# A decoder layer on one core: a fifth pair by seven products in three chunks, and VectorE's queue issued by an account of its time

## The chip, the cores and the metric

The kernel runs on one core of a Trainium2 chip. The metric is the device time of one execution in microseconds. The kernel before takes 1052.63 us (median of three runs, 1052.0 to 1052.91).

The core has five engines that run their own queues in order: TensorE (PE; PEld is its loading of weights), VectorE (DVE), ScalarE (ACT), GpSimd (POOL) and SyncE (SP). SP and POOL mostly issue DMAs here. An engine waits for another by semaphores, and an instruction that waits holds up what stands behind it in the queue of its engine.

## The reference

One decoder layer for 256 tokens of width 2048, in float32:

```python
h   = RMSNorm_pre(x)
p   = h @ W_in                          # A.q A.k A.v | c_q | c_kv | k_rope
A   = dilated sliding-window attention  # 8 heads x 128
B   = multi-head latent attention       # 8 heads
x   = x + RMSNorm_post(concat(A, B) @ W_out)
h   = RMSNorm_pre2(x)
u   = square(relu(h @ W_up))            # W_up is 2048 x 8192
x   = x + RMSNorm_post2(u @ W_down)     # W_down is 8192 x 2048
```

The change is in the up projection, `h @ W_up`.

## The kernel before

**Three products for one.** Each float32 operand is split into a high part `hi` (ScalarE rounds it, line 306 or 310) and a rest `lo` (VectorE subtracts, line 307 or 311). A product is then three matmuls, hi x hi, hi x lo and lo x hi (`three`, line 1048). Each weight tile is loaded from memory by a DMA on SP (line 188), split, and used.

**The up projection** runs over eight chunks `j` of 1024 columns of `W_up`. The 2048 rows of the sum are sixteen blocks `k` of 128 rows. A plain step `k` multiplies one block with both halves of the tokens (`b`) and both halves of the columns (`n`): 4 products, 12 matmuls. Two neighbouring blocks `2k` and `2k+1` form a pair, which is a 2 x 2 by 2 x 2 product of blocks; `seven_products` (line 1053) does it with seven block products, 21 matmuls, in place of eight, 24. For this it needs sums of the weight blocks (called `t` and `u`) and sums of the left blocks (`left_sums`, line 1023, by VectorE and ScalarE, once for the whole projection). The partial results `m` are put together once per chunk (`close`, line 1067) and added to the accumulators (line 967).

`UP_STEPS` (line 105) says what is done in each chunk: `k` is a plain step, `w` a pair whose weight sums VectorE computes on the spot (lines 359 to 364), `p` a prepared pair, whose sums DMAs have computed in memory during the earlier stages (`prepare`, line 583: two copies issued on SP, then four accumulating DMAs on POOL). The sums of a prepared pair come back through the buffer `tu` (1 MB, issued on POOL, line 433) in chunks 0 to 4 and as ordinary loads from chunk 5 on. In chunk 0 all steps are plain, in chunks 1 to 5 pairs 0 to 3 go by seven products (0 and 2 prepared), in chunks 6 and 7 pairs 0 to 2.

The gain of the second norm is multiplied into the weights where they are split (line 310 with a scale, line 311), or, for the blocks that pairs use, into the left side in `left_sums`; `SCALED` (line 110) lists those blocks.

**What sets the order.** All queues are filled in the order in which the Python program issues instructions. `Flow` (line 126) is a planner with a clock of its own: every matmul adds its cost (line 296), and chains of other work (evacuation, sums, prepares) are generators that yield a delay and go on when the clock has come to that time (`pump`). `prepare_all` starts at 50 us of this clock and issues a prepare about every 25. This clock decides only the order in the queues; on the chip each engine goes as fast as its semaphores let it.

`Weights` (line 167) issues load and split of a tile ahead of its use: `get(i)` issues everything up to tile `i + 6` (`W_AHEAD`), but no more than the 8 buffers of `hi` and `lo` allow. Functions hung on a tile (`first`) run when it is issued: the sums of a `w` pair, the loads of `ab` and `tu`. At a chunk's end `up_evac` (line 964) adds `more` to the accumulator on VectorE (967), takes the relu on ScalarE (971), transposes on TensorE (300, tile `rt`) and squares on ScalarE (989). VectorE's addition stands in its queue behind all splits that `get` has issued by then.

Of the kernel before, what the change touches and what calls it, by code (L numbers as in the profile page):

```python
# [26 lines left out]
P = 128  # L27
# [68 lines left out]
SUMS_AHEAD, LOAD_AHEAD = 2, 3  # L96
NUP = FF // CW
# [68 lines left out]

class Weights:


    def __init__(self, nc, pool, split, bufs, ahead):  # L170
        self.nc, self.pool, self.split_fn = nc, pool, split
        self.bufs, self.limit, self.ahead = bufs, bufs, ahead
        self.specs, self.tiles, self.done = [], [], []
        self.first, self.queue = {}, {}

# [46 lines left out]
    def get(self, i):  # L222
        self.emit(i + 1 + self.ahead)
        return self.tiles[i]

# [38 lines left out]
def layer(nc, tc, io):  # L264
    flow = Flow()

# [36 lines left out]
    def split(hi, lo, src, g=None):  # L303
        if g is not None:
            return split_gain(hi, lo, src, g)
        nc.scalar.activation(hi, src, AF.Copy)  # L306
        nc.vector.tensor_tensor(out=lo, in0=src, in1=hi.bitcast(F32), op=OP.subtract)  # L307

    def split_gain(hi, lo, src, g):
        nc.scalar.activation(hi, src, AF.Copy, scale=g)  # L310
        nc.vector.scalar_tensor_tensor(  # L311
# [35 lines left out]
    def seven(load, targets):  # L347
# [3 lines left out]
        st, tt, H = {}, nc.vector.tensor_tensor, 512  # L351
# [159 lines left out]
    def rstd_of(ss, n, width, name, by=None):  # L511
# [4 lines left out]
        nc.vector.tensor_scalar(t, ss, s, e, op0=OP.mult, op1=OP.add)  # L516
# [15 lines left out]
    if N_WARM:  # L532
        zero = mix.tile([P, 512], BF16, name="zero")
        nc.vector.memset(zero, 0.0)
# [28 lines left out]
    def prelude():  # L563
# [14 lines left out]
        nc.vector.reduce_sum(ss0, ss0h, axis=mybir.AxisListType.X)  # L578
# [27 lines left out]
    def tables():  # L606
# [6 lines left out]
        nc.vector.tensor_copy(pos_f, pos_i)  # L613
        ang = pa.tile([P, 2, NB, 96], F32, tag="qkT", bufs=2, name="ang")
        kk_ = pa.tile([P, 2, NB, 96], F32, tag="qkT", bufs=2, name="kk_")
        for w in range(2):
            for b in range(NB):
                nc.vector.tensor_scalar_mul(ang[:, w, b, :], freq[:, w * 96:(w + 1) * 96], pos_f[:, b:b + 1])
            nc.vector.tensor_scalar(kk_[:, w], ang[:, w], 1.0 / (2 * np.pi), 0.25 * w, op0=OP.mult, op1=OP.add)
        yield 1.0  # L620
        nc.vector.tensor_scalar(kk_, kk_, MAGIC, -MAGIC, op0=OP.add, op1=OP.add)
        for c in (C1, C2, C3):
            nc.vector.scalar_tensor_tensor(out=ang, in0=kk_, scalar=-c, in1=ang, op0=OP.mult, op1=OP.add)
        yield 1.0
        nc.vector.tensor_scalar_add(ang[:, 1], ang[:, 1], float(np.pi / 2))
        nc.vector.tensor_scalar(ang, ang, PI_LO, -PI_LO, op0=OP.min, op1=OP.max)
# [3 lines left out]
    def rope(tmp_pool, dst, src, half, nh, first, name):  # L630
# [8 lines left out]
        nc.vector.tensor_tensor(out=t1, in0=src, in1=table(1, 0, w), op=OP.mult)  # L639
        nc.vector.tensor_tensor(out=t2[:, :, :, :half], in0=src[:, :, :, half:], in1=table(0, 0, half), op=OP.mult)  # L640
        nc.vector.tensor_tensor(out=t2[:, :, :, half:], in0=src[:, :, :, :half], in1=table(0, half, w), op=OP.mult)
        nc.vector.tensor_tensor(out=dst, in0=t1, in1=t2, op=OP.add)

    def softmax_pv(wk, dl, sc, bias, scale, v, head, name):
# [4 lines left out]
        for i, (a, e, m) in enumerate(spans):  # L649
            nc.vector.tensor_tensor_reduce(  # L650
                out=s[:, a:e], in0=sc[:, a:e], in1=m, op0=OP.add, op1=OP.max, scale=1.0,
                scalar=-3e38, accum_out=st[:, i:i + 1])
        nc.vector.tensor_scalar_mul(st[:, 2:4], st[:, 0:2], -scale)
# [5 lines left out]
        nc.vector.reciprocal(st[:, 6:8], st[:, 4:6])  # L659
        for i, (a, e, m) in enumerate(spans):  # L660
            nc.vector.tensor_scalar_mul(s[:, a:e], s[:, a:e], st[:, 6 + i:7 + i])
# [13 lines left out]
    def heads_a(qkv, half, hs, after):  # L675
        while any(c in flow.chains for c in after):
            yield 0.5
        for h in hs:
# [6 lines left out]
            nc.vector.tensor_copy(qkT, tp)  # L685
# [78 lines left out]
    def shared_key():  # L764
# [8 lines left out]
        for j in range(2):  # L773
            nc.vector.tensor_copy(krT[j * 64:(j + 1) * 64, j, :], t[j * 64:(j + 1) * 64, :S])
# [9 lines left out]
    def keys(pr, kb):  # L784
# [4 lines left out]
        nc.vector.tensor_copy(kT[:, 2 * pr:2 * pr + 2, :], t.rearrange("p (h s) -> p h s", h=2))  # L789
        yield 0  # L790

    def pair_b(pr, qb, after):
# [9 lines left out]
        nc.vector.tensor_copy(qT, t.rearrange("p (h s) -> p h s", h=2))  # L802
# [5 lines left out]
        nc.vector.tensor_copy(qrT, t[:, :S])  # L808
# [47 lines left out]
    def out_evac(n, b, a):  # L856
# [4 lines left out]
        nc.vector.tensor_tensor(out=yg[b][:, c], in0=a, in1=g_post[:, c], op=OP.mult)  # L861
# [7 lines left out]
    def powers():  # L869
# [6 lines left out]
        nc.vector.reduce_sum(gg, gg4, axis=mybir.AxisListType.X)  # L876
        nc.vector.tensor_scalar_add(pws[:, 3, :], ss0, gg)
        r = rstd_of(pws[:, 3, :], NB, D, "pw")
        yield 2.0
        nc.vector.tensor_single_scalar(out=pw.bitcast(I32), in_=r.bitcast(I32), scalar=0x7F800000, op=OP.bitwise_and)  # L880
        nc.vector.tensor_single_scalar(out=pwi.bitcast(I32), in_=pw.bitcast(I32), scalar=0x7F800000, op=OP.bitwise_xor)
        nc.vector.tensor_scalar_mul(pwi, pwi, 0.5)
        for i, (v, c) in enumerate(((pwi, 1.0 / D), (pwi, EPS), (pw, EPS))):
            nc.vector.scalar_tensor_tensor(out=pws[:, i, :], in0=v, scalar=c, in1=v, op0=OP.mult, op1=OP.mult)
        for b in range(NB):
            for c in (slice(0, CW), slice(CW, D)):
                nc.vector.tensor_scalar_mul(xs[b][:, c], xs[b][:, c], pw[:, b:b + 1])
                yield 1.5

    def residual(b):  # L890

        po, yg, hT = late["po"], late["yg"], late["hT"]
        nc.vector.reduce_sum(ssr[b][:, 0:1], ssy[b], axis=mybir.AxisListType.X)
        r = rstd_of(ssr[b][:, 0:1], 1, D, f"post{b}", (pws[:, 0, b:b + 1], pws[:, 1, b:b + 1]))

        def update(ns):
            cs = [slice(n * 512, (n + 1) * 512) for n in ns]
            for c in cs:
                nc.vector.scalar_tensor_tensor(out=xs[b][:, c], in0=yg[b][:, c], scalar=r, in1=xs[b][:, c],
# [20 lines left out]
        nc.vector.reduce_sum(ssr[b][:, 1:2], ssx[b], axis=mybir.AxisListType.X)  # L920
# [42 lines left out]
    def up_evac(j, b, i, acc, order, more=None):  # L963

        if more is not None:
            yield 0.2
            nc.vector.tensor_tensor(out=acc, in0=acc, in1=more, op=OP.add)
# [8 lines left out]
        if j not in uT:  # L976
# [6 lines left out]
            elif j == 10:  # L983
                t2 = late["up"].tile([P, CW], F32, tag="uT10", bufs=1, name="uT10")
# [28 lines left out]
    def four_sums(q, f):  # L1013

        tt = nc.vector.tensor_tensor
# [315 lines left out]
```

## Time and profile before

| what | value |
|---|---|
| median of three runs | 1052.63 us (1052.0 to 1052.91) |
| the profiled execution | 1053.19 us, its span 1051.4 us |
| TensorE busy | 1038.0 us, 99% of the span |
| VectorE busy | 811.1 us, 77% |
| ScalarE busy | 633.6 us, 60% |
| GpSimd busy | 99.1 us, 9% |
| granted clock of TensorE | 0.998 |
| moved by DMA | 260.81 MB, 248 GB/s on the mean |

The span is the time from the first to the last instruction of the program; the profiled execution's own time is 1.8 us more. A row of a group or of the timeline names the line of the kernel, the engine, the operation, and the tiles as out<-in. In brackets, or behind the bar, stands how long the engine was idle just before it and what ended that wait. A row of the waits gives the sum in us, how many times, and the longest. The matmul durations overlap: what counts is the distance of their starts. An engine that isn't on the chain may be idle at no cost.

### The profile page before, as it was taken

What the parts mean: (1) busy time and instruction counts of PE and PEld (TensorE: products, weight loads), DVE (VectorE), ACT (ScalarE), POOL (GpSimd) and SP (SyncE); (2) the same over time, 40 slices, a digit from 0 to 9 for tenths busy, and PEclk for the clock granted to TensorE, in tenths of its full rate; (3) what the DMA queues carried; (4) which work ended last, traced back from release to release, by engine and by line L of the source; (5) the groups of instructions that cost most, each with busy time, mean ns of one, the idle gap of its engine ahead of it and who ended that gap; (6) DMA issues with size and microseconds to landing.
All of it is one profiled execution on the core that took longest, in us unless ns stands there. A gap on an engine that the chain in (4) does not pass through costs nothing.

```text
span 1051.4 us, 13574 instructions
## 1 busy us (share of the span) xinstructions
PE 1038.0 (99%) x4839; PEld 864.5 (82%) x4839; DVE 811.1 (77%) x1083; ACT 633.6 (60%) x846; POOL 99.1 (9%) x156
## 2 busy tenths in 40 slices
PE   9999999999999999999999999999999999999996
PEld 6888889888888888878888888888888888888885
DVE  6676536567557669988889798887899978989995
ACT  6575436665455566766766766656567564766661
POOL 0011111112001000000100000000000001122100
PEclk9999999999999999999999999999999999999999
DMA  8999889799878295856766666469778767788952
GB/s 291 353 296 295 226 205 318 199 250 303 231 222 260 88 358 179 283 200 225 267 213 235 210 212 199 140 223 325 244 279 303 275 229 257 268 300 319 364 195 82
DMA packets 93572, 260.81 MB, mean 248 GB/s; under 512 B 8768, under 2 KB 13376, under 8 KB 92096
## 3 DMA queue, kind: packets, MB, share of 16 engines
q1 hardware_dynamic: 71776, 190.61, 52.5%
q0 software_dynamic: 21152, 68.69, 23.2%
q8 instruction: 38, 0.62, 0.2%
q10 hardware_dynamic: 576, 0.64, 0.2%
q14 instruction: 30, 0.25, 0.1%
HBM read 244.18 MB, written 39.32 MB: 270 GB/s over the span
## 4 chain that ended last, share of the span: by engine, by line
PE 94%; DVE 2%; DMA 1%; issue 1%; ACT 1%; POOL 0%; DVEq 0%; POOLq 0%; ACTq 0%
PE y L296 26%; PE acc_u L296 23%; PE acc_o L296 8%; PE m L296 7%; PE md L296 5%; PE acc_qk L296 4%; PE acc_v L296 4%; PE acc_cq L296 2%; PE acc_ukv L296 2%; PE acc_q L296 2%; PE acc_k L296 2%; PE acc_uq L296 2%; PE rt L300 1%; PE acc_ckv L296 1%; DMA raw<-in_w_in 1%
## 5 line engine op out<-in xcount | busy, mean ns | idle before, releaser
L307 DVE TENSOR_TENSOR lo<-raw,hi 128x1024 fp32r<-128x1024 f32 (+3 forms) x241 | 269.9, 1137 | 97.7 <-ACT hi L306 97.0
L306 ACT ACTIVATE hi<-raw 128x1024 fp32r<-128x1024 f32 (+3 forms) x241 | 234.9, 988 | 99.6 <-PE y L296 21.4
L296 PE MATMUL y<-hi,uhi 128*128 128x512 f32 x376 | 146.7, 390 | 0.0
L296 PE MATMUL y<-hi,ulo 128*128 128x512 f32 x376 | 146.3, 389 | 0.0
L296 PE MATMUL y<-lo,uhi 128*128 128x512 f32 x376 | 146.3, 389 | 0.0
L296 PE MATMUL acc_u<-hi,hT_hi 128*128 128x512 f32 x356 | 141.7, 398 | 0.0
L296 PE MATMUL acc_u<-hi,hT_lo 128*128 128x512 f32 x356 | 139.2, 391 | 0.4 <-DVE hT_lo L307 0.4
L296 PE MATMUL acc_u<-lo,hT_hi 128*128 128x512 f32 x356 | 138.8, 390 | 0.0
L311 DVE SCALAR_TENSOR_TENSOR lo<-raw,gcol,hi 128x1024 fp32r<-128x1024 f32 x72 | 90.6, 1280 | 17.1 <-ACT hi L310 16.8
L310 ACT ACTIVATE hi<-raw,gcol 128x1024 fp32r<-128x1024 f32 x72 | 81.7, 1149 | 20.9 <-DMA raw<-in_w_up 12.7
L296 PEld LDWEIGHTS y<-hi,ulo 128*128 128x128 f32 x376 | 70.6, 188 | 14.8
L296 PEld LDWEIGHTS y<-hi,uhi 128*128 128x128 f32 x376 | 70.6, 188 | 14.5
L296 PEld LDWEIGHTS y<-lo,uhi 128*128 128x128 f32 x376 | 70.6, 188 | 14.4
L296 PEld LDWEIGHTS acc_u<-hi,hT_lo 128*128 128x128 f32 x356 | 66.8, 188 | 15.1 <-DVE hT_lo L307 0.9
L296 PEld LDWEIGHTS acc_u<-lo,hT_hi 128*128 128x128 f32 x356 | 67.0, 188 | 12.9
L296 PEld LDWEIGHTS acc_u<-hi,hT_hi 128*128 128x128 f32 x356 | 66.9, 188 | 12.8
L296 PE MATMUL m<-hi,st 128*128 128x512 f32 x156 | 56.5, 389 | 0.0
L296 PE MATMUL acc_o<-hi,mixT_hi 128*128 128x512 f32 x128 | 51.8, 405 | 0.0
L307 DVE TENSOR_TENSOR lo<-st_down,hi 128x1024 fp32r<-128x1024 f32 x40 | 48.0, 1219 | 3.9 <-ACT hi L306 3.8
L296 PE MATMUL acc_o<-hi,mixT_lo 128*128 128x512 f32 x128 | 50.2, 392 | 0.0
L296 PE MATMUL acc_o<-lo,mixT_hi 128*128 128x512 f32 x128 | 50.0, 390 | 0.0
L306 ACT ACTIVATE hi<-st_down 128x1024 fp32r<-128x1024 f32 x40 | 42.1, 1053 | 10.8 <-PE y L296 9.4
(329 smaller groups left out, 2041.3 us busy)
## 6 DMA issues: line engine op xcount, KB each, us to landing
raw<-in_w_down SPq DMA_DIRECT2D x88, 512.0 KB, 5.9
raw<-in_w_up SPq DMA_DIRECT2D x86, 512.0 KB, 4.6
raw<-in_w_in SPq DMA_DIRECT2D x55, 512.0 KB, 6.5
raw<-in_w_out SPq DMA_DIRECT2D x32, 512.0 KB, 7.2
ab<-in_w_up POOLq DMA_DIRECT2D x28, 512.0 KB, 5.0
sums<-in_w_up SPq DMA_DIRECT2D x20, 512.0 KB, 7.1
ab_down<-in_w_down POOLq DMA_DIRECT2D x20, 512.0 KB, 6.6
tu<-sums POOLq DMA_DIRECT2D x8, 1024.0 KB, 5.1
```

Of the source, the lines that this page charges most:

```text
L296: nc.tensor.matmul(out, a, b, start=start, stop=stop)
L300: nc.tensor.transpose(out, a, ident)
L306: nc.scalar.activation(hi, src, AF.Copy)
L307: nc.vector.tensor_tensor(out=lo, in0=src, in1=hi.bitcast(F32), op=OP.subtract)
L310: nc.scalar.activation(hi, src, AF.Copy, scale=g)
L311: nc.vector.scalar_tensor_tensor(out=lo, in0=src, scalar=g, in1=hi.bitcast(F32), op0=OP.mult, op1=OP.subtract)
```

## The change

It has three parts.

1. **Steps.** Chunks 2, 3 and 4 take five pairs by seven products (`p0 w1 p2 w3 p4`, pairs 0, 2 and 4 prepared) in a new order, where they took four. Prepared pairs become thirteen where they were ten. The left sums of pair 4 are computed in chunk 1 (`some_sums((4,), 6.0)`, started at its fifth step); blocks 8 and 9 of the left side then carry the gain, so that from chunk 2 on their weights are split without a scale. `st2` becomes twice as large and shares its place with `uT` 10 and 11.
2. **An account of VectorE's time.** `Paced` wraps VectorE: each instruction adds a price to `free`, the time on the planner's clock at which VectorE would be done; `lag()` is how far this is ahead of the clock. All VectorE instructions of the kernel go through it (`vec` for `nc.vector`).
3. **Issue by the account.** From step 8 of chunk 0 to the end of the up projection, tiles may be issued up to 7 ahead, but one that is more than three places ahead is issued only while `lag()` is at most 1.5 us. `more()` tries again after every product and not at each new tile alone.

```diff
+LAG, URGENT = 1.5, 3
...
-for _j in range(1, 6):
-    UP_STEPS[_j] = steps_of("k8 k9 k10 k11 p0 k12 w1 k13 p2 w3 k14 k15")
+UP_STEPS[1] = UP_STEPS[5] = steps_of("k8 k9 k10 k11 p0 k12 w1 k13 p2 w3 k14 k15")
+for _j in range(2, 5):
+    UP_STEPS[_j] = steps_of("k10 k11 k12 p0 w1 p2 k13 w3 p4 k14 k15")
...
-SCALED = {j: range(8) for j in range(1, NUP)}
+SCALED = {j: range(8 if j == 1 else 10) for j in range(1, NUP)}
...
+class Paced:
+    def __init__(self, engine, flow):
+        self.engine, self.flow, self.free = engine, flow, 0.0
+    def __getattr__(self, name):
+        f = getattr(self.engine, name)
+        def call(*args, **kw):
+            out = kw["out"] if "out" in kw else args[0]
+            n = int(np.prod(out.shape[1:]))
+            self.free = max(self.free, self.flow.clock) + 0.952 * (n / 960 + (0.145 if name == "scalar_tensor_tensor" else 0.08))
+            return f(*args, **kw)
+        return call
+    def lag(self):
+        return self.free - self.flow.clock
...
-    def emit(self, upto):
+    def emit(self, upto, must=1 << 30):
         upto = min(upto, self.done.index(False) + self.limit, len(self.specs))
         while len(self.tiles) < upto:
             i = len(self.tiles)
+            if self.lag and i >= must and self.lag() > LAG:
+                return
...
     def get(self, i):
-        self.emit(i + 1 + self.ahead)
+        self.at = i
+        self.more()
         return self.tiles[i]
+    def more(self):
+        self.emit(self.at + 1 + self.ahead, self.at + 1 + URGENT)
...
+    vec = Paced(nc.vector, flow)
...
-            elif j == 10:
-                t2 = late["up"].tile([P, CW], F32, tag="uT10", bufs=1, name="uT10")
+            elif j in (10, 11):
+                if j == 10:
+                    late["uT10"] = late["up"].tile([P, 2 * CW], F32, tag="uT10", bufs=1, name="uT10")
+                t2 = late["uT10"][:, (j - 10) * CW:(j - 9) * CW]
...
             flow.pump()
+            weights.more()
...
-                late["st2"] = late["up"].tile([P, CW], F32R, tag="uT10", bufs=1, name="st2")
+                weights.lag, weights.ahead = vec.lag, W_BUFS - 1
+                late["st2"] = late["up"].tile([P, 2 * CW], F32R, tag="uT10", bufs=1, name="st2")
...
+            if (j, t, b) == (1, 4, 0):
+                flow.start(some_sums((4,), 6.0))
...
     u_last = evac[-4:]
+    weights.lag, weights.ahead = None, W_AHEAD
```

More of the change, by code (lines that the diff above doesn't have):

```diff
@@ L966, in up_evac @@
             yield 0.2
-            nc.vector.tensor_tensor(out=acc, in0=acc, in1=more, op=OP.add)
+            vec.tensor_tensor(out=acc, in0=acc, in1=more, op=OP.add)
             yield 1.4
@@ L1023, in left_sums @@
     def left_sums(kp):
-        up, k, tt = late["up"], 2 * kp, nc.vector.tensor_tensor
+        up, k, tt = late["up"], 2 * kp, vec.tensor_tensor
         f, q = [late["c"][:, i * 512:(i + 1) * 512] for i in range(2)]
@@ L1119, in layer @@
                     flow.pump()
+                    weights.more()
                 if b == NB - 1:
@@ L1196, in half_evac @@
             for b in range(NB):
-                tt, out = nc.vector.tensor_tensor, more[b, n]
+                tt, out = vec.tensor_tensor, more[b, n]
                 tt(out=y[b][n], in0=y[b][n], in1=out, op=OP.add)
@@ L1282, in layer @@
             if g < GT - 1:
-                nc.vector.tensor_tensor(out=y[b][2 + n], in0=y[b][2 + n], in1=more[b, n], op=OP.add)
+                vec.tensor_tensor(out=y[b][2 + n], in0=y[b][2 + n], in1=more[b, n], op=OP.add)
                 if (b, n) == (0, 0):
```

93 lines of the change are left out of this document (47 added, 46 removed).

## The prediction

> **What bounds the kernel now.** I read the page first: busy time, chain.
>
> ```profile
> span 1051.4 us, 13574 instructions
> PE 1038.0 (99%) x4839; PEld 864.5 (82%) x4839; DVE 811.1 (77%) x1083; ACT 633.6 (60%) x846; POOL 99.1 (9%) x156
> ...
> PE 94%; DVE 2%; DMA 1%; issue 1%; ACT 1%; POOL 0%; DVEq 0%; POOLq 0%; ACTq 0%
> ```
>
> TensorE is busy for 99% of the span and is 94% of the chain. So a product removed is time gained, and VectorE's work costs only where it makes TensorE wait. Next the price of a product, from the chain in order of time, in a stretch without a break:
>
> ```profile
> 866.14 32.64 PE y L296 x144
> ```
>
> 32.64 / 144 = 0.2267 us. Then the up projection, cut at the chunks (chunk 1 from 405, chunk 2 from 448, chunk 3 from 490.5), busy time by engine:
>
> ```profile
> core 0: us, PE busy (x) PEld busy (x) DVE busy (x) ACT busy (x) POOL busy (x), PEclk, DMA share, GB/s
> ...
> 405.00:448.00 43.00, 43.00 (x199) 35.61 (x198) 40.70 (x51) 28.89 (x36) 3.24 (x6) 1.00 0.69 240
> 448.00:490.50 42.50, 41.34 (x191) 33.96 (x190) 37.63 (x41) 28.89 (x34) 3.24 (x6) 1.00 0.68 238
> 490.50:533.00 42.50, 42.50 (x197) 35.21 (x196) 35.99 (x38) 28.57 (x33) 3.24 (x6) 1.00 0.68 234
> ```
>
> TensorE has no idle time in chunks 1 and 3, and VectorE is 95% busy in chunk 1 and 85% in chunk 3. The waits of TensorE over the whole span name what is left to gain, and the timeline shows the largest and the one before chunk 6:
>
> ```profile
> PE rt L300 <- ACT r L971: 2.2, 3, 1.2
> ...
> PEld rt L300 <- ACT r L971: 3.5, 3, 1.6
> ...
> 449.89 0.33 PE L300 MATMUL rt<-ident,r 128*128 128x128 f32 x1 [1.16 <-ACT r L971]
> ...
> 618.20 1.28 DVE L311 SCALAR_TENSOR_TENSOR lo<-raw,gcol,hi 128x1024 fp32r<-128x1024 f32 x1
> 619.40 0.68 DVE L307 TENSOR_TENSOR lo<-ab,hi 128x512 fp32r<-128x512 f32 x1
> 620.00 1.89 DVE L967 TENSOR_TENSOR acc_u<-acc_u,c 128x512 f32<-128x512 f32 x3
> ...
> 620.73 0.69 ACT L971 ACTIVATE r<-acc_u,rstd_pre 128x512 f32<-128x512 f32 x1 [4.12 <-DVE acc_u L967]
> ```
>
> Three times the transposes `rt` at a chunk's end wait for the relu `r` (line 971), and that for VectorE's addition at line 967, which stands behind two splits of later tiles (618.20, 619.40). Three holes of 1.2, 0.5 and 0.5 us by TensorE's rows, 3.5 in all by the weight loads': about 2.7 us, 1.3 into chunk 2 and 0.7 each into chunks 6 and 7. Nowhere in the up projection does TensorE wait for a split.
>
> **The change, part by part.** *Products.* A pair of weight rows as two plain steps takes 2 x 12 products, by seven products 7 x 3 = 21. Chunks 2, 3 and 4 get a fifth pair: 9 products fewer, 9 x 0.2267 = 2.04 us off the path. This needs nothing else to go right.
>
> *VectorE's work for the fifth pair.* Groups by form, 405 to 706 us:
>
> ```profile
> L311 DVE SCALAR_TENSOR_TENSOR lo<-raw,gcol,hi 128x1024 fp32r<-128x1024 f32 x52 | 65.2, 1280 | 5.6 <-ACT hi L310 5.3
> L307 DVE TENSOR_TENSOR lo<-raw,hi 128x1024 fp32r<-128x1024 f32 x23 | 27.7, 1220 | 3.7 <-ACT hi L306 3.7
> ...
> L307 DVE TENSOR_TENSOR lo<-raw,hi 128x512 fp32r<-128x512 f32 x9 | 6.2, 683 | 0.0
> ...
> L1028 DVE TENSOR_TENSOR c<-hT_hi,hT_lo 128x512 f32<-128x512 f32 x2 | 1.4, 684 | 0.0
> L1039 DVE TENSOR_TENSOR st<-c,st 128x512 fp32r<-128x512 f32 x2 | 1.4, 684 | 0.0
> ...
> L1030 DVE TENSOR_SCALAR c<-c,gcol 128x256 f32<-128x256 f32 x4 | 1.2, 349 | 0.1
> ...
> L1017 DVE TENSOR_TENSOR c<-c 128x256 f32<-128x256 f32 x2 | 0.9, 426 | 0.1
> L1019 DVE TENSOR_TENSOR c<-c 128x128 f32<-128x128 f32 x2 | 0.6, 292 | 0.1
> ```
>
> A prepared pair has splits of 512 + 3 x 1024: 0.68 + 3 x 1.22 = 4.34 us; it replaces two scaled splits, 2.56. So +1.8 us at most in each of chunks 2 to 4: from 36.0 to 37.8 us of the 41.8 that a chunk has left (42.5 - 0.68). VectorE stays under TensorE there, and I cost it at nothing; should that cover fail, it is 1.8 us in each chunk. Chunks 5 to 7 lose the scaling of two tiles, 0.06 us each: nothing. The fifth pair's quarter sums of the left side (`left_sums(4)`) cost 0.68 + 2 x 0.35 + 0.43 + 2 x 0.29 + 2 x 0.68 = 3.76 us once, and they come in **chunk 1**, from 6 us after its first pair began: where VectorE already has 40.7 of 43.
>
> *Margin in chunk 1.* I compare the end of a split with the first product that reads its `lo`, for the third tile of pair `p2` (the first of the two 1024-wide splits of `tu`) and the last tile of `w3`:
>
> ```profile
> 428.64 2.35 DVE L307 TENSOR_TENSOR lo<-tu,hi 128x1024 fp32r<-128x1024 f32 x2
> ...
> 433.79 1.22 DVE L307 TENSOR_TENSOR lo<-t,hi 128x1024 fp32r<-128x1024 f32 x1
> ...
> 433.15 0.39 PE L296 MATMUL m<-lo,st 128*128 128x512 f32 x1
> ...
> 439.27 0.39 PE L296 MATMUL m<-lo,st 128*128 128x512 f32 x1
> ```
>
> The one ends at 429.85 (428.64 + 1.22) and is read at 433.15, 3.3 us later; the other ends at 435.01 and is read at 439.27, 4.3 later. So 3.76 us more would just fit, if nothing else came later.
>
> *Three more prepares.* Each issues two DMAs on SP (2 x 512 KB) and four on POOL (3 x 256 and 512 KB). Ten now start 25.6 us apart:
>
> ```profile
> L590 SPq DMA_DIRECT2D sums<-in_w_up x10: 522/522/1400, 54.0 to 284.2; - x10
> ```
>
> The order is set by the kernel's own clock (line 296 adds 0.2158 for a product), which I added up: the 11th falls into the output projection, the 12th ahead of chunk 0's loads of rows 3 on, and the 13th's two SP DMAs next to chunk 0's loads of rows 12 and 13. Here is that place, in stretches of 10 us, with ScalarE's waits:
>
> ```profile
> 360.00:370.00 10.00, 9.58 (x49) 7.46 (x48) 8.98 (x15) 5.95 (x12) 1.54 (x2) 1.00 0.26 84
> 370.00:380.00 10.00, 10.00 (x48) 8.27 (x47) 4.64 (x7) 7.74 (x14) 1.54 (x3) 1.00 1.01 371
> 380.00:390.00 10.00, 10.00 (x46) 8.26 (x45) 6.05 (x6) 4.16 (x5) 0.71 (x2) 1.00 1.01 400
> 390.00:400.00 10.00, 10.00 (x46) 8.28 (x45) 9.06 (x17) 6.23 (x8) 0.00 (x0) 1.00 0.68 248
> 400.00:410.00 10.00, 10.00 (x50) 8.27 (x48) 9.42 (x15) 7.38 (x12) 0.00 (x0) 1.00 0.76 234
> ...
> 387.26 1.15 ACT L310 ACTIVATE hi<-raw,gcol 128x1024 fp32r<-128x1024 f32 x1 [2.96 <-DMA raw<-in_w_up]
> ```
>
> The DMA engines are full from 370 to 390, ScalarE waits for a load (2.96 us before 387.26), and from 390 on VectorE works almost without pause into chunk 1. So a load that lands later here moves VectorE's whole queue up to the end of chunk 1. By how much no row shows directly. From above: loads of `raw` issued just ahead of a prepare's SP pair, and those issued just behind one, early in the trace:
>
> ```profile
> raw<-in_w_in SPq DMA_DIRECT2D x4, 512.0 KB, 6.5
> ...
> raw<-in_w_in SPq DMA_DIRECT2D x4, 512.0 KB, 11.8
> ```
>
> 5.3 us later (issued 70.5 to 74.4 and 75.5 to 86). Its size says less: 1 MB at the 371 to 400 GB/s of a full stretch is 2.7. From below: nothing. I take 4, between the size and the measured delay, because POOL's additions of the 12th prepare go at the same place. VectorE's pauses from 390 to 410 (0.94 + 0.58) take back 1.5. At the last tile of `w3`: 4 - 1.5 + 3.76 - 4.3 = **2.0 us of new hole**; with no delay 0, with 5.3 and no pause taken back 4.8.
>
> POOL's queue also carries the four `pow` of the two norms; it is idle before them, and the longest of the added entries issues in 1.2 us. I cost this at nothing; a landing that came late there would delay the norm by as much.
>
> ```profile
> L597 POOL DMA_DIRECT2D sums<-sums x10: 1156/1172/1198, 76.5 to 322.7; - x10
> ...
> 350.36 0.57 POOL L517 TENSOR_TENSOR rstd_post<-t_post,neg_half 128x1 f32<-128x1 f32 x1 [26.42 <-DVE t_post L516]
> ```
>
> *The buffer of the prepared sums.* `tu` is one buffer, and now no plain step stands between `w1` and `p2` in chunks 2 to 4.
>
> ```profile
> tu<-sums POOLq DMA_DIRECT2D x8, 1024.0 KB, 5.1
> ```
>
> Between its last read for `p0` and its first for `p2` VectorE has `w1`'s sums (1.22 + 2 x 0.68), its splits (4.34) and two splits of `p2` (0.68 + 1.22): 8.8 us, over the 5.1 that the transfer takes. Nothing; without that cover each pair would wait for what the transfer runs over.
>
> *Order of VectorE's queue.* A tile more than three places ahead is now issued only if VectorE's account is at most 1.5 us behind, so fewer splits stand ahead of the additions at line 967. Bounds: 0 to 2.7 us gained. I take 1.4, the holes into chunks 6 and 7, where VectorE has time and only the order is at fault; into chunk 2 it arrives with no lead, so that hole stays. A new wait behind the limit would be a split issued too late, but three tiles of a pair are 3 x 21 x 0.2267 / 4 = 3.6 us of products ahead.
>
> The account (Paced) prices 1024 elements at 0.952 x (1024/960 + 0.08) = 1.09 us of the kernel's clock, which is 1.15 us of the chip's (x 0.2267/0.2158). Two such splits in a row took 2.35 us above, so the second added 1.13: the price is right where VectorE doesn't wait. What the account leaves out is waits for a load.
>
> [...]
>
> **Sum:** -2.04 - 1.4 + 2.0 = -1.4 us on the profiled execution, which took 1053.19 (1.8 around its span), so 1051.8. The median of the runs, 1052.63, is 0.56 lower: **1051.2**, 0.14% less.
>
> **The rivals.** *No hole in chunk 1* (0.32). The loads land in time or VectorE's pauses absorb the shift: -2.04 - 1.4, or -4.7 with all three holes gone: 1047.9 to 1049.2. For it: 3.76 is under 4.3, and 1 MB of `ab` loads, behind the 13th prepare's additions in POOL's queue, would move out of the full stretch. Against it: the full DMA stretch.
>
> *VectorE becomes the bound in chunk 1* (0.16), slower: the 13th prepare delays the loads by the measured 5.3 us, nothing is taken back, hole 4.8, and VectorE reaches the chunk's end late, so no order helps: -2.04 + 4.8 = +2.8, 1055.4. It decides once the delay exceeds 1.5 + 4.3 - 3.76 + 2.04 = 4.1 us with no gain at the ends. For it: 95% in the row of chunk 1. Against it: the pauses.
>
> *The order doesn't change* (0.14): VectorE waits for loads, which the account doesn't count, so it is taken as on time, splits pass the limit and stand ahead of the additions; the three holes stay: -2.04 + 2.0 = 1052.6. For it: the wait of 2.96 above. Against it: VectorE's idle time ahead of scaled splits is only 5.6 us over seven chunks.
>
> **How the numbers follow.** The forecast's own case has 0.38, with 1050.2 to 1053.0. About 0.2% (2.1 us) is what a measurement of this kernel can tell from no change: faster is below 1050.5, slower above 1054.7. Faster: 0.32 + 0.06 of the forecast = 0.38. Slower: 0.13 of VectorE's case, 0.03 of the forecast, 0.04 of the case without a new order, where chunks 2 to 4 then fail their cover: 0.20. Same: 0.29 of the forecast, 0.03 of VectorE's case, 0.10 of the last: 0.42. The range of 8 in 10 is 1048.6 to 1055.2, from no hole to nearly the full one.
>
> **What would show it.** Right: 4830 instructions on PE; a wait of TensorE for `lo` between 420 and 445, some 2 us in all; VectorE over 98% busy in chunk 1; ScalarE's waits for `raw` longer after 380; no `rt` wait into chunks 6 and 7. Wrong: no wait for `lo` in chunk 1, or waits in chunks 2 to 4, or in the norm ahead of 370.

## The result, and the profile after

The changed kernel takes **1079.19 us** (median of 4 runs, 1077.52 to 1080.6), the kernel before beside it 1052.34. The ratio is **1.0257, 95% interval 1.0244 to 1.0270**: slower by 27 us, where the prediction had 1051.2 and a range up to 1055.2. The profiled execution's span is 1078.3 us, 26.9 more than before.

The page of the changed kernel, busy time and chain:

```profile
span 1078.3 us, 13609 instructions
PE 1045.4 (97%) x4830; PEld 865.7 (80%) x4830; DVE 819.1 (76%) x1097; ACT 637.7 (59%) x854; POOL 110.9 (10%) x171
...
PE 77%; DVE 10%; DMA 6%; issue 3%; ACT 3%; POOL 0%; DVEq 0%; POOLq 0%; SPq 0%; ACTq 0%
```

The nine products are gone (4830 for 4839), but TensorE's share of the chain fell from 94% to 77%; VectorE, DMA and ScalarE have the rest. Its waits:

```profile
PE rt L331 <- ACT r L1002: 16.2, 8, 7.7
PE acc_u L327 <- DVE c L182: 3.1, 3, 1.4
PE acc_u L327 <- DVE lo L182: 1.9, 4, 0.5
```

The wait of `rt` for the relu `r`, 2.2 us before, is 16.2, in single waits of up to 7.7; new are waits for `close` (`c`) and short ones for splits (`lo`). (Line 1002 is 971 of before, 331 is 300, 327 is 296; all VectorE work now has line 182, in `Paced`.)

Where the time lies, I read from the starts of the first transposes `rt` at the end of each chunk; their differences are in us, chunk 0 with what stands ahead of it (from the first product of `w_ukv` on). So a hole into a chunk counts in the column of the chunk before it. The last column runs from the first product of the down projection to the end of the span; that product comes 2.7 us ahead of chunk 7's mark (3.2 in e3 and e6, 5.0 in e7), so the two columns overlap by as much. The experiments below are in the same table.

```
                         chunk 0     1     2     3     4     5     6     7   down projection
before                     201.1  44.7  42.8  42.7  42.7  43.4  44.1  43.5   345.1
after                      212.1  45.9  49.1  49.3  45.1  43.3  44.4  43.9   344.8
e1 prepares only           212.4  45.9  42.7  42.7  42.7  43.4  44.1  43.4   344.8
e2 prepares late           201.2  48.3  57.8  49.1  44.8  43.3  44.4  43.9   344.9
e3 steps only              211.3  50.1  48.0  47.9  43.7  43.3  44.0  44.0   345.4
e4 account only            201.1  46.5  42.8  42.7  43.0  43.4  44.1  43.5   345.2
e5 prepares fast           201.2  45.6  48.5  50.1  43.7  43.2  44.4  43.9   344.9
e6 three ahead             209.3  45.6  44.1  42.6  44.0  42.7  45.0  44.2   348.0
e7 fast, three ahead       201.1  45.6  44.2  42.7  45.8  42.7  47.4  46.1   347.6
e8 sums by raw             211.7  45.8  45.5  46.9  42.9  43.3  44.4  43.9   344.9
e9 four pairs, 3 first     201.2  43.4  42.7  42.7  42.7  43.4  44.1  43.4   345.1
e10 before, limit closed   201.1  43.4  42.7  42.7  42.7  42.7  50.0  43.4   345.1
e12 e9, short ends         201.1  43.5  42.7  42.7  42.7  42.7  43.5  45.0   345.1
```

After against before: +11.0 in chunk 0 with the hole at its end, +1.2, +6.3, +6.6, +2.4 in chunks 1 to 4, +0.6 in chunks 5 to 7, -1.0 ahead of the table and -0.3 behind it: 26.8 of the 26.9.

**The first place: into chunk 1.** In 10 us stretches of the changed kernel (columns as in the prediction), and the waits of ScalarE and TensorE in its timeline:

```profile
370.00:380.00 10.00, 10.00 (x47) 8.27 (x46) 1.32 (x2) 3.83 (x9) 0.00 (x0) 1.00 1.01 280
380.00:390.00 10.00, 9.05 (x39) 6.81 (x39) 6.53 (x7) 5.18 (x6) 4.10 (x5) 1.00 1.05 365
390.00:400.00 10.00, 9.58 (x43) 7.61 (x42) 3.42 (x4) 3.09 (x3) 1.92 (x3) 1.00 1.04 329
400.00:410.00 10.00, 7.05 (x30) 5.17 (x28) 8.11 (x15) 5.54 (x7) 1.22 (x1) 1.00 1.06 365
...
392.89 1.15 ACT L341 ACTIVATE hi<-raw,gcol 128x1024 fp32r<-128x1024 f32 x1 [5.72 <-DMA raw<-in_w_up]
396.65 1.15 ACT L341 ACTIVATE hi<-raw,gcol 128x1024 fp32r<-128x1024 f32 x1 [2.61 <-DMA raw<-in_w_up]
...
409.43 0.63 ACT L1069 ACTIVATE hT_hi<-c 128x512 fp32r<-128x512 f32 x1 [1.26 <-DVE c L182]
...
414.53 0.66 ACT L1002 ACTIVATE r<-acc_u,rstd_pre 128x512 f32<-128x512 f32 x1
...
415.25 1.12 PE L331 MATMUL rt<-ident,r 128*128 128x128 f32 x4 [7.69 <-ACT r L1002]
```

The DMA engines were full from 370 to 390; now they are full from 370 to 410, and moved only 280 GB/s in the first 10 us where they had moved 371. ScalarE waits 5.72 us for one load (2.96 was its longest wait for one before). The relu at chunk 0's end needs nothing but its product, which was done at about 405; it starts at 414.53, since it stands in ScalarE's queue behind the splits that waited (and behind left sums, the row at 409.43). TensorE waits 7.69 us for it. The loads of this place, before (issued 369.5 to 373) and after (369 to 373):

```profile
raw<-in_w_up SPq DMA_DIRECT2D x5, 512.0 KB, 7.0
```

```profile
raw<-in_w_up SPq DMA_DIRECT2D x5, 512.0 KB, 12.9
```

and a little later, before (377.5 to 386) and after (381 to 389):

```profile
raw<-in_w_up SPq DMA_DIRECT2D x6, 512.0 KB, 8.9
```

```profile
raw<-in_w_up SPq DMA_DIRECT2D x5, 512.0 KB, 13.1
```

The last ones are also issued 3 to 5 us later, because buffers come free later. Counted in order, the tile of weights that ScalarE split at 387.26 before is the second-last of chunk 0; now the second-last is split at 396.65, 9.4 us later, though the chunk began a microsecond earlier. (The row at 392.89 is the tile ahead of it.)

**The second place: into chunks 3 and 4.** The loads issued from 488 to 495 us, the end of chunk 2, in the changed kernel:

```profile
raw<-in_w_up SPq DMA_DIRECT2D x3, 512.0 KB, 9.8
tu<-sums POOLq DMA_DIRECT2D x1, 1024.0 KB, 8.5
ab<-in_w_up POOLq DMA_DIRECT2D x2, 512.0 KB, 11.3
```

and its timeline there, POOL, ScalarE, VectorE and TensorE:

```profile
488.58 0.53 POOL L464 DMA_DIRECT2D tu<-sums  x1 [8.69 <-DVE lo L182]
489.10 1.05 POOL L408 DMA_DIRECT2D ab<-in_w_up  x2
...
497.38 0.63 ACT L337 ACTIVATE hi<-raw 128x512 fp32r<-128x512 f32 x1 [4.66 <-DMA raw<-in_w_up]
499.94 1.06 ACT L337 ACTIVATE hi<-raw 128x1024 fp32r<-128x1024 f32 x1 [1.93 <-DMA raw<-in_w_up]
...
498.05 0.69 DVE L182 TENSOR_TENSOR lo<-raw,hi 128x512 fp32r<-128x512 f32 x1 [3.79 <-ACT hi L337]
501.04 1.22 DVE L182 TENSOR_TENSOR lo<-raw,hi 128x1024 fp32r<-128x1024 f32 x1 [2.29 <-ACT hi L337]
502.18 2.27 DVE L182 TENSOR_TENSOR c<-m,c 128x512 f32<-128x512 f32 x3
...
508.82 2.48 DVE L182 TENSOR_TENSOR acc_u<-acc_u,c 128x512 f32<-128x512 f32 x4
...
505.23 0.51 PE L327 MATMUL acc_u<-hi,hT_hi 128*128 128x512 f32 x1 [1.35 <-DVE c L182]
510.28 0.66 PE L331 MATMUL rt<-ident,r 128*128 128x128 f32 x4 [3.38 <-ACT r L1002]
```

Pair 4 is now the last of the chunk and the last reader of `tu`. So the load of `tu` for the next chunk waits in POOL's queue until 488.58, and the two loads of `ab` stand behind it, although VectorE's last split that reads `ab` had ended at 482.0. Then 1 MB of `tu`, 1 MB of `ab` and the plain loads of the next chunk's first pair run together and take 8.5 to 11.3 us. That pair's splits stand in VectorE's queue ahead of this chunk's `close` (502.18) and additions (508.82), and wait 3.79 and 2.29 us for those loads. The next chunk's accumulators use the banks that `close` reads, so TensorE waits for it too (1.35 us at 505.23).

**A third part: the clock.** In stretches that begin with these holes, the column behind POOL is the clock granted to TensorE:

```profile
411.00:419.00 8.00, 3.75 (x12) 3.15 (x13) 7.39 (x11) 5.83 (x9) 0.00 (x0) 0.57 0.96 282
510.00:515.00 5.00, 4.72 (x18) 3.85 (x19) 4.35 (x6) 3.71 (x6) 1.06 (x2) 0.66 0.19 33
558.00:566.00 8.00, 6.46 (x21) 5.38 (x22) 5.60 (x8) 4.89 (x8) 1.58 (x3) 0.57 0.33 109
...
560.88 0.63 PE L327 MATMUL acc_u<-lo,hT_hi 128*128 128x512 f32 x1
561.30 0.63 PE L327 MATMUL acc_u<-hi,hT_lo 128*128 128x512 f32 x1
```

At each of the three large holes the clock is granted at half for a while: in stretches of half a microsecond it is 0.50 from 412.0 to 418.5, from 511.0 to 514.0 and from 559.0 to 565.0. Products then start 0.43 us apart in place of 0.2267. Twenty products do so, which is 4.0 us; the transposes among them are slower too (four took 1.12 us at 415.25 and 0.60 at 419.39). The four transposes and nine products right behind the holes take 4.14, 4.14 and 4.76 us (from 415.25, 510.28 and 559.53), where the same work takes 2.52 at the full clock (from 419.39). So some 5.5 us of the 27 are the clock's, and no wait shows them. In the kernel before every stretch of the up projection had 1.00.

### The profile page after: what moved, and what is told of

The parts are those of the page before. It is cut to its first block, busy times and chain, and to the rows that moved or that the text cites. A ratio compares the mean times of both kernels' runs of the same rounds, so it can differ in the third digit from the quotient of the medians.

```text
span 1078.3 us, 13609 instructions
## 1 busy us (share of the span) xinstructions
PE 1045.4 (97%) x4830; PEld 865.7 (80%) x4830; DVE 819.1 (76%) x1097; ACT 637.7 (59%) x854; POOL 110.9 (10%) x171
## 4 chain that ended last, share of the span: by engine, by line
PE 77%; DVE 10%; DMA 6%; issue 3%; ACT 3%; POOL 0%; DVEq 0%; POOLq 0%; SPq 0%; ACTq 0%
PE y L327 25%; PE acc_u L327 10%; PE acc_o L327 8%; DVE lo L182 6%; PE md L327 5%; DMA raw<-in_w_up 5%; PE acc_qk L327 4%; PE acc_v L327 4%; PE m L327 3%; PE acc_ckv L327 2%; PE acc_ukv L327 2%; PE acc_q L327 2%; PE acc_cq L327 2%; PE acc_k L327 2%; DVE c L182 2%
## 5 line engine op out<-in xcount | busy, mean ns | idle before, releaser
L182 DVE TENSOR_TENSOR lo<-raw,hi 128x1024 fp32r<-128x1024 f32 (+3 forms) x253 | 282.8, 1135 | 106.5 <-ACT hi L337 105.5
L337 ACT ACTIVATE hi<-raw 128x1024 fp32r<-128x1024 f32 (+3 forms) x253 | 246.0, 987 | 109.2 <-PE y L327 21.5
L327 PE MATMUL acc_u<-hi,hT_hi 128*128 128x512 f32 x338 | 137.7, 407 | 4.1 <-DVE c L182 3.1
L327 PE MATMUL acc_u<-lo,hT_hi 128*128 128x512 f32 x338 | 134.1, 397 | 1.9 <-DVE lo L182 1.9
L327 PE MATMUL acc_u<-hi,hT_lo 128*128 128x512 f32 x338 | 133.8, 396 | 0.4 <-DVE hT_lo L182 0.4
L182 DVE SCALAR_TENSOR_TENSOR lo<-raw,gcol,hi 128x1024 fp32r<-128x1024 f32 x60 | 75.3, 1280 | 23.6 <-ACT hi L341 23.4
L341 ACT ACTIVATE hi<-raw,gcol 128x1024 fp32r<-128x1024 f32 x60 | 68.3, 1149 | 29.4 <-DMA raw<-in_w_up 23.4
L327 PEld LDWEIGHTS acc_u<-lo,hT_hi 128*128 128x128 f32 x338 | 64.8, 192 | 15.7 <-DVE lo L182 3.6
L327 PEld LDWEIGHTS acc_u<-hi,hT_lo 128*128 128x128 f32 x338 | 64.6, 191 | 14.7 <-DVE hT_lo L182 0.8
L327 PE MATMUL m<-hi,st 128*128 128x512 f32 x174 | 63.0, 389 | 0.0
L337 ACT ACTIVATE hi<-st_down 128x1024 fp32r<-128x1024 f32 x40 | 42.1, 1052 | 11.0 <-PE y L327 9.5
```

The costliest lines, as they stand in the source:

```text
L182: return f(*args, **kw)
L327: nc.tensor.matmul(out, a, b, start=start, stop=stop)
```

## The experiments

The theory after the result: the late prepares delay chunk 0's loads (first place), and the order of VectorE's queue at the chunk's end, with loads that bunch there, makes the second. Rivals: the account alone, the new order of the steps alone, the fifth left sums.

**e1, three more prepares in the kernel before.** Nothing else changes; the sums of the three are never read.

```diff
-PREP = [(j, k) for j in UP_STEPS for w, k in UP_STEPS[j] if w == "p"]
+PREP = [(1, 0), (1, 2), (5, 0), (5, 2), (2, 0), (2, 2), (2, 4), (3, 0), (3, 2), (3, 4), (4, 0), (4, 2), (4, 4)]
```

> The kernel before with thirteen prepares in the place of ten; the sums of three of them (pair 4 in chunks 2, 3 and 4) are computed and never read. Theory of the loads (the 12th and 13th prepare fall into the full DMA stretch of chunk 0, loads land late, and the relu at chunk 0's end stands in ScalarE's queue behind splits that wait for them): a hole of about 8 us into chunk 1 and some 3 us of small ones in chunk 0, so 1063 us. Rival (the slowdown is all in the order of the steps and VectorE's queue): 1052 to 1053, no hole into chunk 1.

1063.93 us, ratio 1.0107 (1.0090 to 1.0123). TensorE's waits from 396 to 420 us:

```profile
PE rt L300 <- ACT r L971: 6.3, 1, 6.3
PE acc_u L296 <- DVE lo L311: 1.1, 2, 0.6
```

The first place is there whole, with neither the fifth pair nor the account: chunk 0 costs 212.4 as in the changed kernel, and chunks 2 to 7 are those of before. The theory of the loads holds for it, by size and place.

**e2, the last two prepares begun later,** in the changed kernel.

```diff
+            if jk in PREP[-2:]:
+                yield max(0.0, (395.0 if jk == PREP[-2] else 425.0) - flow.clock)
             yield from prepare(*jk)
```

> The changed kernel, with the last two prepares (pairs 2 and 4 of chunk 4) begun no earlier than 395 and 425 us of the kernel's own clock, in chunks 1 and 2. Theory of the loads: the hole of 7.9 us into chunk 1 and the small ones before it go, the holes into chunks 3 and 4 stay: 1079 - 11 = 1068 us. Rival: about 1079.

1079.69 us, ratio 1.0264 (1.0248 to 1.0279). Chunk 0 is back at 201.2, but the whole time isn't less: chunks 1 and 2 take 2.4 and 8.7 us more than in the changed kernel. VectorE's timeline in chunk 2:

```profile
475.00 1.23 DVE L182 TENSOR_TENSOR t<-ab 128x1024 f32<-128x1024 f32 x1 [8.70 <-DMA ab<-in_w_up]
```

The same mechanism at another place: a prepare beside `tu` and `ab`, and VectorE waits 8.7 us for `ab`. The hole was moved, not removed; my expected 1068 missed this.

**e3, the changed steps and prepares without the limit by the account,** 6 ahead as before.

```diff
-                weights.lag, weights.ahead = vec.lag, W_BUFS - 1
```

> The changed kernel without the limit by the account: tiles are issued up to 6 ahead again, whatever VectorE's lag; five pairs, thirteen prepares, order of steps as changed. Theory of the order by the account (7 ahead and a lag that doesn't know of late loads put the next chunk's splits ahead of the close and the additions): the holes into chunks 3 and 4, some 6.5 us each, go or shrink by half, the one into chunk 1 stays: 1066 to 1072 us. Rival (the new order of the steps, three plain steps ahead of the first pair, makes them): 1079 or more.

1078.10 us, ratio 1.0247 (1.0232 to 1.0263). My theory said that the account's limit lets the splits pass; the holes into chunks 3 and 4 are almost as long without it (48.0, 47.9), and the one into chunk 2 longer. So the account isn't what puts the splits ahead of the additions: the old rule does so too.

**e4, the account and its limit alone,** with the steps and prepares of before.

```diff
-for _j in range(2, 5):
-    UP_STEPS[_j] = steps_of("k10 k11 k12 p0 w1 p2 k13 w3 p4 k14 k15")
+for _j in range(2, 5):
+    UP_STEPS[_j] = UP_STEPS[1]
...
-SCALED = {j: range(8 if j == 1 else 10) for j in range(1, NUP)}
+SCALED = {j: range(8) for j in range(1, NUP)}
...
-            if (j, t, b) == (1, 4, 0):
-                flow.start(some_sums((4,), 6.0))
```

> The changed kernel with the steps of the kernel before in all chunks (four pairs, ten prepares, no fifth left sums): only the account, the limit and 7 ahead are new. Theory of the loads and of the order together: no hole into chunk 1; with four plain steps ahead of the first pair the next chunk's splits are ready, so 1051 to 1054 us, holes into chunks 2, 6 and 7 somewhat smaller. Rival (the account alone does the harm): 1060 or more.

1054.63 us, ratio 1.0029 (1.0019 to 1.0039): slower by 0.3%. The wait of `rt` in the up projection is 3.3 us where it was 2.2, most of it into chunk 2 (46.5 for 44.7), and the holes into chunks 6 and 7 stay. The time is just over the 1051 to 1054 that I expected, and those holes didn't cost less. The account gains nothing and costs a little; it isn't the cause of the 27 us.

**e5, the prepares closer together,** in the changed kernel.

```diff
-D_PREP = (50.0, 24.0, 12.0)
+D_PREP = (50.0, 18.0, 9.0)
```

> The changed kernel with the prepares closer together (18 us of the kernel's clock for one, 9 between its parts, where it was 24 and 12), so that the thirteenth ends where the tenth ended before, ahead of the norm. Theory of the loads: no full DMA stretch beyond that of the kernel before at chunk 0, the hole into chunk 1 falls from 7.9 to about 1 us and the small ones go, and none comes back in chunk 2, where the late prepares had made one: 1079 - 10 = 1069 us. Rival (three more prepares cost their time wherever they stand): 1075 or more, with waits in the projections.

1070.54 us, ratio 1.0171 (1.0154 to 1.0188). The first place goes here without coming back in the up projection (201.2), but some 5 us are paid ahead of it: TensorE's waits from 5 to 360 us are

```profile
PE pT_a L331 <- DVE s_a L182: 3.0, 2, 2.2
PE acc_qk L327 <- ACT hi L337: 1.8, 2, 1.2
```

where the kernel before had 1.0 in all. In e7, with the same prepares, only some 2 us are paid there, so this part varies between executions.

**e6, the limit always closed:** nothing more than three places ahead. In this kernel and in e7 the buffer `ab` of chunk 7's first pair is given to another tile before the pair's last splits read it (here the squares are written to it from 676.89 on, the splits read at 680.48 and 682.99), so part of that pair is computed from other data; times from chunk 6 on are read with care.

```diff
-LAG, URGENT = 1.5, 3
+LAG, URGENT = -1000.0, 3
```

> The changed kernel with the limit always closed: no tile more than three places ahead is issued in the up projection, whatever the account says. Theory of the queue's order (the close and the additions at a chunk's end stand behind splits of the next chunk's first pair, which wait for loads): the close comes at once, the holes into chunks 3 and 4 (6 to 7 us each with the waits for the close) go, that into chunk 1 stays or shrinks a little: 1064 to 1068 us. Rival (the loads are late there in any order, and TensorE waits for the splits in place of the close): 1075 to 1080.

1069.37 us, ratio 1.0162 (1.0131 to 1.0193), just over the 1064 to 1068 expected. The large holes into chunks 3 and 4 go: 44.1 and 42.6 for 49.1 and 49.3, though `tu` and `ab` are still loaded together there (489.73 and 490.25). So it is the order in the queue that turns late loads into those holes. The first place stays (209.3), as a wait of 2.75 us for a split in chunk 0, with a granted clock of 0.51 from 401 to 408. What comes instead is smaller. TensorE's waits from 410 to 600 us:

```profile
PE m L327 <- DVE lo L182: 4.8, 6, 1.7
```

Not one wait for `r`, six for splits of the pairs.

**e7, e5 and e6 together.**

```diff
-LAG, URGENT = 1.5, 3
+LAG, URGENT = -1000.0, 3
...
-D_PREP = (50.0, 24.0, 12.0)
+D_PREP = (50.0, 18.0, 9.0)
```

> Both at once: prepares closer together and the limit always closed. If the two causes are separate and all there is: 1079 - 10 - 13 = 1056 us, and less if the holes of the kernel before go too (1052.3 - 2.0 - 2.7 = 1047.6 at best). If the fifth left sums make a hole in chunk 1 as the prediction had it, it shows here as a wait of TensorE for lo between 410 and 445 us. Rival (a third cause): over 1060.

1064.84 us, ratio 1.0118 (1.0100 to 1.0137); the expected 1056 was missed, and over 1060 was to mean a third cause. Both places are gone, but the chunks with five pairs take 44.2, 42.7 and 45.8 us, not the 42.1 that their products ask for. VectorE in chunk 2:

```profile
470.09 1.22 DVE L182 TENSOR_TENSOR t<-ab 128x1024 f32<-128x1024 f32 x1 [1.61 <-DMA ab<-in_w_up]
```

The sums of `w3` wait for `ab`, and the split of `p2`'s last tile stands behind them; with a lead of only three tiles, TensorE then waits 1.74 us for it. The rest of this run's loss lies in chunks 6 and 7 and behind them, where it isn't comparable. Between 410 and 445, where the fifth left sums are computed, TensorE waits three times for `lo`, 1.2 us in all. The longest, 0.68 us at 437.26, is for a split that stands in VectorE's queue behind two of their additions (434.78 and 435.38). In e5, with the same prepares and sums but without the closed limit, there is no wait for `lo` there at all.

**e8, the kept sums of pair 4 as ordinary loads,** so that `tu` is free from pair 2 on.

```diff
-                if j < 5:
+                if j < 5 and k != 4:
```

> The changed kernel, but the kept sums of pair 4 come as ordinary loads on SP and not through the single buffer tu, so tu is free from pair 2 on and its next load need not wait for the end of the chunk. Theory of the bunched loads (tu for the next chunk's first pair can start only when pair 4 has read it, and then lands together with ab and the plain loads): chunks 2 and 3, 49 us each in the changed kernel against 42.7 before, fall to 44 to 46, in all 1070 to 1074 us. Rival (three plain steps ahead of the first pair are too few in any case): chunks 2 and 3 stay at 48 to 50, 1077 to 1080 us.

1073.82 us, ratio 1.0207 (1.0188 to 1.0227). Chunks 2 and 3 fall from 49.1 and 49.3 to 45.5 and 46.9, and no wait for `close` is left from 420 to 600 us, only

```profile
PE rt L331 <- ACT r L1002: 7.6, 4, 3.3
```

POOL now issues the loads of `ab` as soon as VectorE has read the buffer, 8 us earlier than in the changed kernel:

```profile
480.43 0.53 POOL L408 DMA_DIRECT2D ab<-in_w_up  x1 [1.27 <-DVE lo L182]
```

So the bunching through `tu`, and through what stands behind its load in POOL's queue, makes about half of the second place; the additions behind the next chunk's splits remain.

**e9, the short distance without the fifth pair:** the kernel before, with three plain steps ahead of the first pair in chunks 2 to 4.

```diff
+    UP_STEPS[_j] = steps_of("k8 k9 k10 k11 p0 k12 w1 k13 p2 w3 k14 k15" if _j in (1, 5)
+                            else "k8 k9 k10 p0 k11 w1 k12 p2 k13 w3 k14 k15")
```

> The kernel before, with the steps of chunks 2, 3 and 4 in the order k8 k9 k10 p0 k11 w1 k12 p2 k13 w3 k14 k15: still four pairs and ten prepares, but three plain steps ahead of the first pair and two behind the last, as in the changed kernel. Rival of e8 (the short distance from the last pair of a chunk to the first of the next makes the holes): chunks 2 to 4 at 45 us or more, 1058 us or more. Theory of the bunched loads: tu is read last in the middle of the chunk, so at most the holes of the kernel before, 1052 to 1055 us.

1051.04 us, ratio 0.9989 (0.9980 to 0.9999). No hole in chunks 2 to 4, and the one into chunk 2 of the kernel before is gone (43.4 for 44.7). The rival falls for this kernel: with four pairs, three plain steps ahead of the first are enough. Against the changed kernel it has one pair fewer, another order behind the first pair, and a last pair that isn't read from `tu`; which of these matters, this run doesn't tell apart. Timed again in more rounds, beside e12:

> The same kernel as in the run with four pairs and three plain steps first, timed in more rounds, since its gain was near what can be told. If the gain is the hole into chunk 2 that went (1.3 us of 1052): ratio 0.9985 to 0.999. If it was chance: 1.000.

1051.22 us, ratio 0.9992 (0.9982 to 1.0002). A gain of about a microsecond, at the edge of what can be told.

**e10, the steps of before with the limit closed** from chunk 1 to the first steps of chunk 6. It is made from the changed kernel, with the steps and prepares of before and without the account's limit; what is added:

```diff
+            if (j, t, b) == (1, 6, 0):
+                weights.lag = lambda: 1e9
+            if (j, t, b) == (6, 3, 0):
+                weights.lag = None
```

> The steps and prepares of the kernel before, and from step 6 of chunk 1 to step 3 of chunk 6 no tile more than three places ahead is issued; elsewhere 6 ahead, without the account. Theory of the queue's order: the holes into chunk 2 (1.3 us) and chunk 6 (0.7 us) go and none comes: 1050.3 to 1050.8 against 1052.3. Rival (the splits come too late behind the closed limit): 1053 or more.

1056.56 us, ratio 1.0038 (1.0025 to 1.0051). The holes into chunks 2 and 6 go as expected (43.4 and 42.7), but chunk 6 then takes 50.0: a split comes too late, TensorE waits 2.1 us for it, and the granted clock in the 4 us behind is 0.57; at the chunk's end it waits for `close` and the relu too. From 643 to 649 and from 649 to 653 us, and its waits from 350 to 706:

```profile
643.00:649.00 6.00, 3.87 (x17) 2.89 (x16) 5.11 (x6) 3.62 (x5) 0.41 (x1) 1.00 0.10 15
649.00:653.00 4.00, 4.00 (x12) 3.16 (x11) 4.00 (x5) 3.79 (x5) 0.66 (x2) 0.57 0.89 313
...
PE acc_u L327 <- DVE lo L182: 2.1, 1, 2.1
PE rt L331 <- ACT r L1002: 1.5, 1, 1.5
PE acc_u L327 <- DVE c L182: 0.6, 1, 0.6
```

**e12, e9 with 3 ahead only around the ends of chunks 5 and 6.**

```diff
+            if j in (5, 6) and t == len(steps) - 2:
+                weights.ahead = 3
+            elif j in (6, 7) and (t, b) == (0, 1):
+                weights.ahead = W_AHEAD
```

> That kernel, and in the last two steps of chunks 5 and 6 tiles are issued only 3 ahead, until the second half of the next chunk's first step. Theory of the queue's order: the additions at line 967 come ahead of the next chunk's splits, the holes into chunks 6 and 7 (0.7 us each) go: 1.4 us under the run beside it. Rival (opening the limit again brings the splits too late, as in the run with the limit closed up to chunk 6): a wait for lo in chunk 6 or 7, 1 us or more above it.

1051.23 us, ratio 0.9992 (0.9983 to 1.0002), the same as the run beside it. The holes into chunks 6 and 7 go (42.7 and 43.5), and no wait for `lo` comes; in their place one of 1.4 us stands in chunk 7 (45.0), at 668.25, ahead of the second set of transposes of chunk 6's end:

```profile
PE rt L300 <- ACT r L971: 1.4, 1, 1.4
```

## Why the prediction was wrong

**Products (-2.04): right in count, and hidden.** Nine products went. In e6, chunk 3 takes 42.6 us with a hole of about half a microsecond, 42.7 before without one: the gain is there, but only where nothing else is late.

**Three more prepares (new hole of 2.0, bounds 0 to 4.8): the mechanism was right, the size and the place were not.** This is the step that failed first. I took a delay of 4 us for the loads, at most the 5.3 measured beside one early prepare. Here two prepares met `tu`, `ab` and the catching up of chunk 0's loads, and the second-last tile of the chunk was split 9.4 us later by ScalarE's rows, from a chunk that began a microsecond earlier. The estimate from bytes went wrong because the rate itself fell: 280 GB/s at a DMA share of 1.01, where it had been 371. And I followed the delay only through VectorE's splits into chunk 1, where I had the margins of 3.3 and 4.3 us. It ended first at a reader that I hadn't listed, the relu in ScalarE's queue behind the delayed splits: 7.69 us into chunk 1, with waits for `lo` ahead of it. Chunk 0 cost 11.0 in all. e1 shows that this is the prepares' doing alone.

**The fifth left sums (3.76 us): nearly no hole of theirs was seen.** The margin in chunk 1 held in e5, where the loads came in time: no wait for `lo`, with VectorE 98% busy (44.78 of 45.60 us), as foreseen. With the closed limit of e7 they have a part in one wait of 0.68 us. In the changed kernel TensorE had been held up by then.

**Chunks 2 to 4 at no cost: wrong, the second step that failed.** I compared busy times (37.8 of 41.8 us), and checked `tu` only between `p0` and `p2`. Between `p4` and the next chunk's `p0` I did not look: there `tu` comes free late, the loads of `ab` stand behind its load in POOL's queue, and both run together with the plain loads. VectorE had the time but stood idle, waiting for loads, with `close` and the additions behind it. It cost 6.3 and 6.6 us in chunks 2 and 3, and much of the 2.4 in chunk 4 is the halved clock at the last hole (4.76 us for work that takes 2.52 at the full clock). e8 removes about half of it by the buffer, e6 nearly all of it by the order.

**The order of the queue (-1.4): not gained.** e4 shows the outcome that my rival for this foresaw: with the account alone, chunks 5 and 6 take as long as before, and the whole costs 0.3% more. The rival's reason, that the account doesn't count waits for loads, is not shown by it. It fits into chunk 2, where VectorE had waited 2.12 us for a late tile (before 442.94) and two splits stand between `close` and the additions; into chunk 6 VectorE works without a pause from 606.24 on, and one split still stands ahead of them. What I had against that rival, little idle time of VectorE ahead of scaled splits, was read from a kernel whose loads were in time and says nothing of the changed one. Two splits in a row took 2.35 us in e4 (at 599.71), as in the prediction's row, so the price isn't shown to be at fault.

**POOL at nothing: nearly right.** The last of the four `pow` did wait for a prepare, 11.80 us, and ran at 381.69 where it had run at 378.33, but nobody needed it so early. The loads of `ab` did move behind the 13th prepare's additions, as my first rival had it (from 379.62 and 380.17 to 390.93 and 391.49), but not out of the full stretch: that now reached to 410.

```profile
381.69 0.56 POOL L548 TENSOR_TENSOR rstd_pre<-t_pre,neg_half 128x1 f32<-128x1 f32 x1 [11.80 <-DMA sums<-in_w_up]
```

**The range.** Its upper end was the largest value of one term. Three terms failed together. Late loads were behind two of them, the prepares and chunks 2 to 4; the third, the order, fails in e4 without any added transfer. And the holes cost some 5.5 us more by the clock, which I had not counted. One small reading was off as well: before the change TensorE does wait once for a split in the up projection, 0.4 us for `hT_lo` in chunk 0.

What stays open: why e5 pays 5 us in the projections and e7 only 2; and whether the fifth pair can gain its 2 us at all. The second place would need another buffer or order, and the prepares another place, and every place that was tried for them cost something. No version that keeps the fifth pair came near the kernel before. e9, without it, is about 1 us faster than that kernel, at the edge of what can be told. It also stays open why the splits pass the account's limit.

## What to carry to other kernels

A delay must be followed through every in-order queue that it enters, to all that stands behind it: here the costly one was a relu of 0.66 us, for which TensorE waited 7.69, behind splits that had waited for loads. Busy time under the bound says that work fits, not that it is ready in time; look at the moment when buffers come free, and at what starts loading then. Where the DMA engines were already full, the added transfers cost more than their bytes at the old rate: from 370 to 380 us the rate was 280 GB/s with them and 371 without.

## What the runs showed of the hardware that was not expected

The clock granted to TensorE fell at some short holes and not at others. In the changed kernel it was 0.57 and 0.66 in the stretches shown, at holes with single waits of 7.69, 3.38 and 3.41 us; at the first and the last of them it stood at 0.50 before the wait had ended (from 412.0, with TensorE at work again from 415.25, and from 559.0, at work again from 559.53). In e10 it was 0.57 in the 4 us behind a single wait of 2.1 us. In chunk 4 of e7 it was 0.51 behind one of 1.81 us, and at the end of chunk 3 of e8 it was 1.00 behind one of 3.14 us:

```profile
560.88 0.50 PE L327 MATMUL m<-lo,st 128*128 128x512 f32 x1 [1.81 <-DVE lo L182]
561.50:565.00 3.50, 3.50 (x10) 2.75 (x9) 3.50 (x5) 1.77 (x3) 1.21 (x3) 0.51 0.69 246
...
553.00 0.65 PE L331 MATMUL rt<-ident,r 128*128 128x128 f32 x4 [3.14 <-ACT r L1002]
554.00:562.00 8.00, 8.00 (x43) 6.62 (x42) 5.10 (x6) 7.45 (x12) 1.59 (x3) 1.00 0.64 239
```

In the kernel before, behind its holes of 1.2 us and less, it was 1.00 (from 449.5 to 457, from 621 to 628 and from 664 to 672). So these runs give no length of a wait at which it falls.

Transfers that add into memory (the prepares' additions) took more of the DMA engines' time than their bytes suggest. The rows of POOL's queue (q0) and SP's (q1) give packets, MB and the share of the 16 engines' time. In the kernel before, from 380 to 390 us, q0 has only the plain loads of `tu` and `ab`; in the changed kernel, from 370 to 380, only additions:

```profile
q0 software_dynamic: 415, 2.06, 52.4%
...
q1 hardware_dynamic: 415, 2.06, 57.3%
q0 software_dynamic: 388, 0.71, 43.5%
```

The plain loads moved 2.06 MB in 52.4% of the time, the additions 0.71 MB in 43.5%: about 2.4 times as long for a byte. SP's queue, with the loads of `raw` and the 13th prepare's copies, had little more than half of the engines left beside them. So the same 10 us, with the engines full in both kernels (a DMA share of 1.01), moved 371 GB/s without them and 280 GB/s with them.
